# The seam between two transformer blocks: a ring of staging tiles, earlier reordered copies, and zero stores in another stage

## The chip, the cores and the metric

The kernel runs on one NeuronCore of a Trainium2 chip. A NeuronCore has a matrix engine (TensorE; PE in the profile, PEld for its weight loads), three engines for everything else (VectorE = DVE, ScalarE = ACT, GpSimd = POOL) and SyncE (SP), which here only issues transfers; ACT issues some as well. [...] The metric is device time in microseconds (us); lower is better.

## The reference, cut to what matters

One sequence of 512 tokens, 1024 wide, runs through a first network of two layers and then a hybrid layer, all in float32. What lies around the change:

```python
x = first_block(...)            # each layer ends: x = x + sigmoid(norm(x) @ Wg) * (p[i] @ Wp); then a norm
h = rms_norm_2(x, norm_g)       # the hybrid layer ("second block")
proj = h @ w_in                 # q, k, v of a sparse attention, and r, k, v, wd, ad, gate of an RWKV-7 mixer
p = p + shift_mu * (prev - p)   # token shift: prev is p one token earlier; for r, k, v, wd, ad
w = w0 + tanh(wd) @ w_up        # low-rank decay, rank 64
a = sigmoid(a0 + ad @ a_up)     # low-rank learning rate, rank 64
state = state * w_t + (state @ -kk_t) (kk_t * a_t) + v_t k_t      # per token, 8 heads of 64 x 64
```

The recurrence over tokens is computed in chunks of 64; within a chunk it needs the inverse of a unit triangular matrix per head.

## The kernel before, in words

Every float32 product is made of three products of halves: a weight unit is loaded by SP (`fetch`, line 162), rounded by ACT to `whi` (line 147), and the rest `wlo` is taken by DVE or POOL (line 148, by `N.lo`). Activations are split likewise into a high and a low tile. Lines 188 to 190 are the matmuls of `cols` (output transposed), line 205 those of `rows`.

**Token order.** The first block keeps its tokens in a permuted order (token mod 8 outermost), the second needs them in natural order. `natural` (line 322) makes reordered copies of the activations: 16 copies of 128x512, eight on ACT and eight on DVE (line 330).

**Stage A, the end of the first block** (lines 1526 to 1529, inside the `with` of pool `pn1`, for the second layer): after the last norm, `rwkv_proj_first` projects r, k, v of heads 0 to 3 (`hh` = 0) in permuted order, six passes of 48 matmuls. Each pass is evacuated by ACT (line 796), scaled by mu on DVE (797) and subtracted on POOL (798) into two large tiles, and eight stores of 384 KB (line 812) write them to the DRAM scratch `d_raw[0]`, undoing the permutation. Then `rwkv_lowrank` multiplies out the low-rank inputs (`cols` of `r_wa`), reorders and shifts them (lines 752 to 758), and for decay and learning rate and four token tiles does a float32 matmul over 65 rows (64 plus a row of ones; 769), tanh on ACT (771), a scaling on DVE (773) and a store on ACT's queue to `d_low` (774), with two output tiles in turn. r of heads 4 to 7 (`hh` = 1) follows.

**Stage B, the start of the second block** (lines 1540 to 1554): `rwkv_consts` loads two constants (728), casts them (730), clears a tile (733), and stores it eight times as zeros into the scratch `d_t` (736), which later holds the block inverses with zeros around them. k and v of heads 4 to 7 follow, then `natural`, then eight calls of `rwkv_local` (two halves of the heads, four token tiles), the local part of each chunk: each loads `low` from `d_low` (837) and r, k, v from `d_raw` (841), rounds the decay (221, `rt_lh`) and begins its matmuls with the cumulative sums into the banks `xa` (865). All of them read scratch that stage A wrote.

**The solve** (`rwkv_solve`, line 957): 31 steps of a forward substitution on DVE, 54 pairs of a product (967) and a subtraction (969), then four stores to `d_t` (972), which `rwkv_applied` loads back (995) for its matmuls (1003). `products` (line 1581) is the rest of the second block's matmul work: sparse-attention keys, gates, and query rows (`nsa_rows`, whose transposes are line 1229 and whose low parts DVE takes at line 1233).

**What sets the order.** The program is written with a tile framework that puts each engine's instructions in order itself: it picks what is ready in its own model of time, and among ready ones what the program emits first. So work emitted late can run early. On the chip every engine then runs its list strictly in order. A tile of a pool with `bufs` = n waits until the tile n allocations earlier is no longer in use; memory of a closed pool is waited for tile by tile.

## Time and profile before

| | |
|---|---|
| median of 3 runs | 1230.6 us (1230.04 to 1232.56) |
| the profiled execution | 1231.49 us |
| its span in the trace | 1229.7 us |
| mean granted TensorE clock | 0.969 of full speed |
| PE busy | 1141.6 us (93%) |
| DVE, ACT, POOL busy | 847.8, 623.7, 401.8 us |

The span is the traced part of one execution; 1.8 us of its time lie around it. Matmuls are pipelined and overlap in the listing, so a matmul's pace is read from the distance of starts, not from its duration. Where a row ends in brackets, they hold the engine's idle time before it and what ended it. In timelines of SP and ACT, "SPq" and "ACTq" rows are transfers being issued.

### The profile page before, as it was taken

The page shows a single profiled execution, that of the slowest core. Times are in us where ns is not written, and L with a number is a line of the kernel's source. Part 1 is how long each engine was busy: PE and PEld are TensorE (multiplying, and loading weights), DVE is VectorE, ACT ScalarE, POOL GpSimd, SP SyncE. Part 2 cuts the span into 40 slices and gives each one's busy share as a digit, 9 for nine tenths or more (in the row PEclk, how much of TensorE's full clock was granted, in tenths as well). Part 3 has the DMA queues.
Part 4 walks back from the last instruction along what each step waited for, and adds up shares of the span by engine and source line. Part 5 has one row for each costly group of instructions (what it writes and reads, how often), then busy time and mean ns, then how long its engine had stood idle before and what let it go on. Part 6 is the DMA issues. An engine that isn't in the chain of part 4 may idle for free.

```text
span 1229.7 us, 20522 instructions
## 1 busy us (share of the span) xinstructions
PE 1141.6 (93%) x7176; PEld 1001.5 (81%) x7176; DVE 847.8 (69%) x2097; ACT 623.7 (51%) x1355; POOL 401.8 (33%) x553
## 2 busy tenths in 40 slices
PE   7999999998999989999999999798989799899995
PEld 6898989887889768887877797788889688798884
DVE  6566666657677977886676763398885924788846
ACT  5566565635533566556565543433543223267832
POOL 0021211111200465674311011263444523357841
PEclk9999999999999999999999999899788979999998
DMA  6333333314233210210142436766657543712501
GB/s 247 116 104 103 104 98 95 99 53 141 88 102 90 82 35 1 69 38 32 52 146 66 149 107 205 239 225 180 192 167 175 162 137 103 241 45 78 189 35 69
DMA packets 87041, 143.26 MB, mean 116 GB/s; under 512 B 21525, under 2 KB 52245, under 8 KB 86938
## 3 DMA queue, kind: packets, MB, share of 16 engines
q1 hardware_dynamic: 72344, 133.49, 34.3%
q10 hardware_dynamic: 14018, 6.36, 2.0%
q0 software_dynamic: 576, 2.10, 0.6%
q8 instruction: 57, 0.93, 0.3%
q14 instruction: 46, 0.38, 0.1%
HBM read 114.12 MB, written 27.79 MB: 115 GB/s over the span
## 4 chain that ended last, share of the span: by engine, by line
PE 61%; DVE 18%; DMA 6%; ACT 6%; issue 5%; POOL 3%; SPq 2%; ACTq 0%; DVEq 0%; POOLq 0%
PE mm L205 24%; PE mm L188 5%; PE mm L189 5%; PE mm L190 5%; PE sc L205 3%; PE mm L216 2%; PE u L677 1%; PE tr L492 1%; DVE KT L967 1%; PE tr L670 1%; DVE big L969 1%; PE ch L1003 1%; PE tr L318 1%; DMA rkv<-d_raw 1%; PE u L205 1%
## 5 line engine op out<-in xcount | busy, mean ns | idle before, releaser
L205 PE MATMUL mm<-whi,act 128*128 128x256 f32 (+2 forms) x1344 | 357.4, 324 | 8.7 <-DVE x L347 3.3
L205 PE MATMUL mm<-wlo,act 128*128 128x256 f32 (+2 forms) x896 | 287.5, 321 | 0.4 <-POOL wlo L148 0.4
L205 PEld LDWEIGHTS mm<-whi,act 128*128 128x128 f32 x1344 | 240.9, 195 | 30.2 <-DVE x L347 5.6
L205 PEld LDWEIGHTS mm<-wlo,act 128*128 128x128 f32 x896 | 174.9, 195 | 10.3 <-POOL wlo L148 0.6
L147 ACT CAST whi<-wraw 128x1024 fp32r<-128x1024 f32 (+1 forms) x128 | 133.3, 1043 | 91.5 <-PE mm L205 36.8
L205 PE MATMUL mm<-whi,half 128*128 128x256 f32 (+1 forms) x448 | 145.6, 326 | 3.6 <-DVE half L222 3.6
L148 DVE TENSOR_TENSOR wlo<-wraw,whi 128x1024 fp32r<-128x1024 f32 x87 | 109.7, 1263 | 52.0 <-ACT whi L147 50.0
L148 POOL TENSOR_TENSOR wlo<-wraw,whi 128x1024 fp32r<-128x1024 f32 (+2 forms) x41 | 99.6, 2434 | 132.0 <-DVE rs_y L237 69.9
L188 PE MATMUL mm<-act,whi 128*128 128x512 f32 x312 | 125.4, 402 | 2.7 <-DVE b_qn L547 2.7
L190 PE MATMUL mm<-act,wlo 128*128 128x512 f32 x312 | 124.4, 399 | 0.0
L205 PEld LDWEIGHTS mm<-whi,half 128*128 128x128 f32 x448 | 87.8, 196 | 10.2 <-DVE half L222 4.5
L484 POOL TENSOR_SCALAR a_P<-a_P,a_rd 128x256 f32<-128x256 f32 x64 | 32.9, 517 | 156.6 <-DVE a_rd L483 143.9
L189 PE MATMUL mm<-half,whi 128*128 128x512 f32 x200 | 79.1, 396 | 0.0
L188 PEld LDWEIGHTS mm<-act,whi 128*128 128x128 f32 x312 | 59.6, 191 | 14.4 <-issue 3.6
L190 PEld LDWEIGHTS mm<-act,wlo 128*128 128x128 f32 x312 | 59.5, 191 | 12.0
L663 POOL TENSOR_SCALAR b_P<-b_P,b_rd 128x512 f32<-128x512 f32 x64 | 45.5, 715 | 54.8 <-DVE b_rd L662 44.2
L660 ACT ACTIVATE b_P<-sc,b_mn 128x512 f32<-128x512 f32 x64 | 44.1, 690 | 21.5 <-DVE b_mn L657 13.5
L657 DVE TENSOR_REDUCE b_mn<-sc 128x1 f32<-128x512 f32 x64 | 43.5, 684 | 10.9 <-PE sc L655 10.4
L478 DVE CUSTOM_DVE_ANT_0 a_P<-sc,a_bias 128x256 f32<-128x256 f32 x64 | 26.1, 422 | 34.7 <-PE tr L492 20.1
L222 DVE TENSOR_TENSOR b_pl<-tr,b_ph 128x512 fp32r<-128x512 f32 x64 | 43.3, 683 | 6.0 <-ACT b_ph L221 5.3
L1359 POOL TENSOR_SCALAR n_P<-n_P,b_rd,n_gl 128x128 f32<-128x128 f32 (+3 forms) x64 | 39.0, 616 | 25.5 <-DVE b_rd L1357 6.4
L189 PE MATMUL mm<-act,whi 128*128 128x512 f32 x112 | 45.3, 404 | 0.0
(391 smaller groups left out, 2836.5 us busy)
## 6 DMA issues: line engine op xcount, KB each, us to landing
wraw<-in_wstream SPq DMA_DIRECT2D x133, 512.0 KB, 3.6
a_bias<-in_bias SPq DMA_DIRECT2D x16, 384.0 KB, 3.0
rkv<-d_raw SPq DMA_DIRECT2D x16, 384.0 KB, 4.9
d_raw<-act SPq DMA_DIRECT2D x8, 384.0 KB, 5.7
xf<-x SPq DMA_DIRECT2D x4, 512.0 KB, 3.7
d_low<-low ACTq DMA_DIRECT2D x8, 256.0 KB, 2.5
d_t<-rkv SPq DMA_DIRECT2D x8, 256.0 KB, 4.1
low<-d_low SPq DMA_DIRECT2D x8, 256.0 KB, 3.3
```

The lines of the kernel that those rows point to most:

```text
L147: nc.scalar.copy(hi[:, :m], raw[:, :m])
L148: self.lo.tensor_tensor(lo[:, :m], raw[:, :m], hi[:, :m].bitcast(F32), op=OP.subtract)
L188: nc.tensor.matmul(ps, lhsT=wh[:, kt], rhs=ah[:, kt], start=kt == 0, stop=False)
L189: nc.tensor.matmul(ps, lhsT=wh[:, kt], rhs=al[:, kt], start=False, stop=False)
L190: nc.tensor.matmul(ps, lhsT=wl[:, kt], rhs=ah[:, kt], start=False, stop=kt == KT - 1)
L205: nc.tensor.matmul(ps, lhsT=l, rhs=r, start=i == 0, stop=i == len(ops) - 1)
L222: (eng_lo or nc.vector.tensor_sub)(lo, src, hi.bitcast(F32))
L484: nc.gpsimd.tensor_scalar(w, w, rd, 0.5, op0=OP.mult, op1=OP.mult)
L657: nc.vector.tensor_reduce(mn, ps, axis=AX.X, op=OP.max, negate=True)
L660: nc.scalar.activation(pt, ps, AF.Exp, bias=mn, scale=1.0, accum_out=den)
L663: nc.gpsimd.tensor_scalar(pt, pt, rd, 0.5, op0=OP.mult, op1=OP.mult)
L1359: nc.gpsimd.tensor_scalar(w, w, rd, st["gl"][:, b, gc:gc + 1], op0=OP.mult, op1=OP.mult)
```

## The change

- `rwkv_proj_first` is gone. All passes of heads 0 to 3 and of r of heads 4 to 7 use one ring `pp` of four tiles of 128x512 in `pn1` (two per pass; the name is that of a ring of the gate stage, now shared). Each pass issues its own four stores of 128 KB: 24 for heads 0 to 3 in place of eight of 384 KB.
- `natural` runs right after the projections of heads 0 to 3 are emitted. The low rank, and all of heads 4 to 7, read the natural-order copies; stores of heads 4 to 7 go to contiguous rows.
- The low rank: its loads and constant rows are emitted ahead of the `r_wa` product; the shift is one ACT and one DVE instruction on the product in PSUM; the products run over 128 rows (64 of data, one of ones, the rest zeros, cleared on POOL); three output tiles in turn.
- The zeros are cleared on POOL and stored from `zero_inverses`, called in the first layer's gate loop (`ple` of layer 0) at its second half, token tile 0.
- `rwkv_solve` is a generator: four steps are emitted after each of the first products.

```diff
-        zero = pool.tile([P, 768], F32, name="rkv", bufs=4)
-        nc.vector.memset(zero, 0.0)
+
+    def zero_inverses(self, pool):
+        nc = self.nc
+        zero = pool.tile([P, 512], F32, name="zero", bufs=1)
+        nc.gpsimd.memset(zero, 0.0)
         for t in range(TT):
             for h in range(2):
-                nc.sync.dma_start(out=self.head_rows(self.d_t, t, 4 * h, 4), in_=zero[:, :512].rearrange("p (h n) -> p h n", h=4))
+                nc.sync.dma_start(out=self.head_rows(self.d_t, t, 4 * h, 4), in_=zero.rearrange("p (h n) -> p h n", h=4))
...
-        ps = self.cols(("r_wa",), act)
-        raw, d = buf[:, 0], buf[:, 1]
-        nc.scalar.copy(raw.rearrange("p (r t c) -> p t c r", r=8, t=TT), ps.rearrange("p (t c r) -> p t c r", t=TT, r=8))
...
-        nc.vector.tensor_sub(d[:, 1:], raw[:, :S - 1], raw[:, 1:])
-        nc.vector.tensor_scalar(d[:, 0:1], raw[:, 0:1], -1.0, None, op0=OP.mult)
-        nc.vector.scalar_tensor_tensor(d, d, mu, raw, op0=OP.mult, op1=OP.add)
-
+        rest = self.small.tile([P, 1], F32, name="wa_rest", bufs=1)
+        nc.vector.tensor_scalar(rest, mu, -1.0, 1.0, op0=OP.mult, op1=OP.add)
+        ms = []
         for j, (up, row) in enumerate((("decay_up", "decay_w0"), ("iclr_up", "iclr_a0"))):
+            m, one = buf[:, 3 + 2 * j], 64 - 64 * j
+            nc.gpsimd.memset(m[64 - 64 * j:128 - 64 * j], 0.0)
+            nc.sync.dma_start(out=m[64 * j:64 * j + 64], in_=self.a[up])
+            nc.sync.dma_start(out=m[one:one + 1], in_=bass.AP(tensor=self.a[row].tensor, offset=self.a[row].offset, ap=[[S, 1], [1, S]]))
+            l = buf[:, 2 + 2 * j]
+            nc.gpsimd.memset(l[64 - 64 * j:128 - 64 * j], 0.0)
+            nc.gpsimd.memset(l[one:one + 1], 1.0)
+        ps = self.cols(("r_wa",), act)
+        d = buf[:, 0]
+        nc.scalar.mul(d, ps, rest)
+        nc.vector.scalar_tensor_tensor(d[:, 1:], ps[:, :S - 1], mu, d[:, 1:], op0=OP.mult, op1=OP.add)
+
+        for j in range(2):
             l, m = buf[:, 2 + 2 * j], buf[:, 3 + 2 * j]
...
+            nc.scalar.activation(l[w], d[w], AF.Tanh if j == 0 else AF.Copy)
             for t in range(TT):
                 ps = self.bank("sc")
-                nc.tensor.matmul(ps, lhsT=l[0:65, t * P:t * P + P], rhs=m[0:65], start=True, stop=True)
-                th = buf[:, 6 + t % 2]
+                nc.tensor.matmul(ps, lhsT=l[:, t * P:t * P + P], rhs=m, start=True, stop=True)
+                th = buf[:, (1, 6, 7)[(4 * j + t) % 3]]
...
-                for t in range(2 * hh):
+                for t in range(2):
                     for d, a in zip(self.d_raw[hh], r):
-                        o = bass.AP(tensor=d.tensor, offset=d.offset + (1 + 16 * (2 * tp + t)) * 768 + 256 * n, ap=[[768, 16], [64 * 768, 8], [1, 256]])
+                        o = (1 + (16, P)[hh] * (2 * tp + t)) * 768 + 256 * n
+                        o = bass.AP(tensor=d.tensor, offset=d.offset + o, ap=[[[768, 16], [64 * 768, 8]], [[768, P]]][hh] + [[1, 256]])
                         nc.sync.dma_start(out=o, in_=a[:, t])
...
                 nc.vector.tensor_tensor(tv, tv, o, op=OP.subtract)
+            yield
...
+                        if (hf, t) == (1, 0):
+                            N.zero_inverses(pool)
...
-                    rest = N.rwkv_proj_first(act, N.rwkv_mu(pool, 0, 0, 3, "mu0"))
+                    ring = lambda n, tp: [pool.tile([P, 512], F32, name="pp", bufs=4).rearrange("p (t n) -> p t n", t=2) for _ in range(2)]
+                    N.rwkv_proj(act, 0, "rkv", N.rwkv_mu(pool, 0, 0, 3, "mu0"), ring)
+                    act = N.natural(act)
                     N.rwkv_lowrank(pool.tile([P, 8, S], F32, name="low", bufs=1), act)
-                    N.rwkv_proj(act, 1, "r", N.rwkv_mu(pool, 1, 0, 1, "mu1"), lambda n, tp: [a[:, tp] for a in rest])
+                    N.rwkv_proj(act, 1, "r", N.rwkv_mu(pool, 1, 0, 1, "mu1"), ring)
...
-                act = N.natural(act)
...
-            N.rwkv_solve(chn, *sv)
+            solve = N.rwkv_solve(chn, *sv)
...
             for n, _ in enumerate(products()):
+                for _ in range(4 if n < 9 else 0):
+                    next(solve, None)
                 tail(n)
```

## Rows read from the trace of the kernel before

**Rows 1.** Busy time by stretch; columns: us, five engines, granted clock, DMA share, GB/s
```profile
720.00:743.00 23.00, 23.00 (x194) 23.00 (x192) 10.47 (x11) 8.25 (x11) 6.08 (x4) 1.00 0.44 131
...
787.00:793.00 6.00, 0.00 (x0) 0.00 (x0) 0.00 (x0) 0.35 (x2) 0.00 (x0) 0.87 0.80 246
...
797.00:937.00 140.00, 128.69 (x938) 118.82 (x938) 114.89 (x286) 60.88 (x191) 66.72 (x76) 0.87 0.60 187
```

**Rows 2.** Timeline of PE around 787 us: first matmul after the gap, and the pace
```profile
793.11 0.58 PE L865 MATMUL xa<-rt_lh,tri 128*128 128x256 f32 x1 [6.81 <-ACT rt_lh L221]
793.49 0.41 PE L205 MATMUL mm<-wlo,act 128*128 128x256 f32 x1
...
797.97 0.41 PE L205 MATMUL mm<-wlo,act 128*128 128x256 f32 x1
```

**Rows 3.** Timeline of SP, 774 to 789 us
```profile
774.63 0.33 SPq L686 DMA_DIRECT2D k_k<-in_k_k  x1
780.54 6.34 SPq L736 DMA_DIRECT2D d_t<-rkv  x8
...
788.65 0.43 SPq L837 DMA_DIRECT2D low<-d_low  x1
```

**Rows 4.** Timeline of ACT, 764 to 780 us
```profile
764.74 0.33 ACTq L774 DMA_DIRECT2D d_low<-low  x1
...
769.27 0.60 ACT L771 ACTIVATE low<-sc 128x512 f32<-128x512 f32 x1 [2.92 <-DMA d_low<-low]
770.03 1.20 ACT L330 CAST act<-half 128x512 fp32r<-128x512 f32 x1 [0.16 <-DMA d_raw<-act]
...
771.13 7.63 ACT L330 CAST act<-half 128x512 fp32r<-128x512 f32 x7
```

**Rows 5.** Timeline of PE, first matmuls of stage B
```profile
769.92 0.38 PE L205 MATMUL mm<-whi,act 128*128 128x256 f32 x1 [2.39 <-ACT low L771]
...
770.98 0.40 PE L205 MATMUL mm<-whi,half 128*128 128x256 f32 x1
...
773.95 0.41 PE L205 MATMUL mm<-wlo,act 128*128 128x256 f32 x1
```

**Rows 6.** Groups by line, 713 to 770 us: count, busy us, mean ns, idle before
```profile
L798 POOL TENSOR_TENSOR act<-act,act 128x512 f32<-128x512 f32 x8 | 11.2, 1399 | 77.1 <-DVE act L797 42.7 <-DVE rs_t L245 34.3
...
L769 PE MATMUL sc<-low 65*128 65x512 f32 x16 | 8.0, 598 | 0.4 <-ACT low L771 0.4
...
L797 DVE TENSOR_TENSOR act<-mm,mu 128x512 f32<-128x512 f32 x7 | 4.8, 688 | 4.8 <-ACT act L796 4.8
...
L796 ACT COPY act<-mm 128x512 f32<-128x512 f32 x7 | 4.1, 586 | 7.9 <-PE mm L205 7.9
```

**Rows 7.** Line 802's stores of 128 KB: issue ns min/median/max, time to landing
```profile
L802 SPq DMA_DIRECT2D d_raw<-act x8: 518/556/616, 757.7 to 767.6; - x8
...
DMA to landing us min/median/max: 2.3/3.7/7.1
```

**Rows 8.** SP's own waits, 690 to 1010 us: total, times, longest
```profile
SPq L162 <- DVE wlo L148: 19.2, 6, 7.8
```

**Rows 9.** Busy time in the first layer's gate stage, columns as in rows 1
```profile
320.00:330.00 10.00, 10.00 (x50) 8.38 (x49) 3.34 (x5) 4.47 (x9) 2.58 (x2) 1.00 0.01 2
```

**Rows 10.** Timelines of DVE, POOL and PE during the solve
```profile
956.88 0.47 DVE L967 TENSOR_TENSOR KT<-big,big 128x160 f32<-128x160 f32 x2
957.26 2.67 DVE L969 TENSOR_TENSOR big<-big,KT 128x160 f32<-128x160 f32 x2
...
957.31 2.52 POOL L148 TENSOR_TENSOR wlo<-wraw,whi 128x1024 fp32r<-128x1024 f32 x1 [4.84 <-ACT whi L147]
...
983.73 1.09 PE L1229 MATMUL mm<-ident,st 128*128 128x128 f32 x4 [8.35 <-DVE half L1233]
```

**Rows 11.** The chain that ended last: start us, us, what; around the solve
```profile
930.46 1.04 PE mm L1150 x4
...
988.33 6.83 DMA big<-d_t
```

More of the change, by code (lines that the diff above doesn't have):

```diff
@@ L755, in rwkv_lowrank @@
                                               ap=[[1, P], [1, 1]]))
-        nc.vector.tensor_sub(d[:, 1:], raw[:, :S - 1], raw[:, 1:])
-        nc.vector.tensor_scalar(d[:, 0:1], raw[:, 0:1], -1.0, None, op0=OP.mult)
-        nc.vector.scalar_tensor_tensor(d, d, mu, raw, op0=OP.mult, op1=OP.add)
+        rest = self.small.tile([P, 1], F32, name="wa_rest", bufs=1)
+        nc.vector.tensor_scalar(rest, mu, -1.0, 1.0, op0=OP.mult, op1=OP.add)
+        ms = []
         for j, (up, row) in enumerate((("decay_up", "decay_w0"), ("iclr_up", "iclr_a0"))):
-            l, m = buf[:, 2 + 2 * j], buf[:, 3 + 2 * j]
-            nc.scalar.activation(l[0:64], d[64 * j:64 * j + 64], AF.Tanh if j == 0 else AF.Copy)
-            nc.vector.memset(l[64:65], 1.0)
-            nc.sync.dma_start(out=m[0:64], in_=self.a[up])
-            nc.sync.dma_start(out=m[64:65], in_=bass.AP(tensor=self.a[row].tensor, offset=self.a[row].offset,
-                                                        ap=[[S, 1], [1, S]]))
+            m, one = buf[:, 3 + 2 * j], 64 - 64 * j
[10 more added lines that the diff above has]
+        for j in range(2):
+            l, m = buf[:, 2 + 2 * j], buf[:, 3 + 2 * j]
+            w = slice(64 * j, 64 * j + 64)
+            nc.scalar.activation(l[w], d[w], AF.Tanh if j == 0 else AF.Copy)
             for t in range(TT):
                 ps = self.bank("sc")
-                nc.tensor.matmul(ps, lhsT=l[0:65, t * P:t * P + P], rhs=m[0:65], start=True, stop=True)
-                th = buf[:, 6 + t % 2]
+                nc.tensor.matmul(ps, lhsT=l[:, t * P:t * P + P], rhs=m, start=True, stop=True)
+                th = buf[:, (1, 6, 7)[(4 * j + t) % 3]]
                 nc.scalar.activation(th, ps, AF.Tanh, scale=0.5)
@@ L798, in rwkv_proj @@
                 nc.gpsimd.tensor_tensor(r[0], r[0], r[1], op=OP.subtract)
-                for t in range(2 * hh):
+                for t in range(2):
                     for d, a in zip(self.d_raw[hh], r):
-                        o = bass.AP(tensor=d.tensor, offset=d.offset + (1 + 16 * (2 * tp + t)) * 768 + 256 * n, ap=[[768, 16], [64 * 768, 8], [1, 256]])
+                        o = (1 + (16, P)[hh] * (2 * tp + t)) * 768 + 256 * n
+                        o = bass.AP(tensor=d.tensor, offset=d.offset + o, ap=[[[768, 16], [64 * 768, 8]], [[768, P]]][hh] + [[1, 256]])
                         nc.sync.dma_start(out=o, in_=a[:, t])
-    def rwkv_proj_first(self, act, mu):
-        raw = [self.act_tile(self.act, j, F32).rearrange("p k n -> p (k n)") for j in range(2)]
-        full = [a[:, :TT * 768].rearrange("p (t n) -> p t n", t=TT) for a in raw]
-        self.rwkv_proj(act, 0, "rkv", mu, lambda n, tp: [a[:, 2 * tp:2 * tp + 2, 256 * n:256 * n + 256] for a in full])
-        for t in range(TT):
-            for d, a in zip(self.d_raw[0], full):
-                o = bass.AP(tensor=d.tensor, offset=d.offset + (1 + 16 * t) * 768, ap=[[768, 16], [64 * 768, 8], [1, 768]])
-                self.nc.sync.dma_start(out=o, in_=a[:, t])
-        return [a[:, TT * 768:].rearrange("p (a t n) -> p a t n", a=2, t=2) for a in raw]
     def rwkv_params(self, pool, hh):
```

## The prediction

> **What bounds the kernel now.** I read the busy time by stretch first, then PE's timeline in the stretches where PE is not full, then the lists of the engines named there. In stage A PE is full: 194 matmuls in 23.0 us at full clock, 0.119 us each, with every other engine under half busy [rows 1]. So in stage A PE is the pace, and work of other engines hides. At the seam there are two holes. PE's first matmul of stage B waits 2.39 us for the low rank's tanh on ACT, whose PSUM bank it inherits, and that tanh had waited 2.92 us for a store to free its output tile [rows 4, 5]. Then PE stands still 6.81 us for `rt_lh`, the first instruction of `rwkv_local` [rows 2]: between 787 and 793 us no engine but ACT does anything [rows 1]. The reader is to see in SP's list why: `low` is issued at 788.65, behind the eight zero stores that occupy SP from 780.54 for 6.34 us, and these start only at 780.54 although the transfer before them went out at 774.63 [rows 3], since DVE clears their tile behind its share of the reordered copies. [...]
>
> Behind the seam, from 797 to 937 us, PE is busy for 128.7 of 140 us and DVE for 114.9 [rows 1]; both matter, and PE draws on attention work that is emitted late and needs nothing of the local part. Then DVE is given to the solve, and PE waits once more, 8.35 us, for a DVE instruction that stands behind solve steps [rows 10].
>
> **The change part by part.** All against the profiled execution, 1231.49 us.
>
> *Zeros out of stage B.* The 6.81 us wait goes if `low` is there in time. Without the zeros SP goes from `k_k` (774.63, issue 0.33) to two parameter loads and `low`; before, those two took from 786.88 (end of the zeros) to 788.65, 1.8 us, so `low` is issued at 776.7 at the latest. From its issue to the first matmul passed 4.5 us (788.65 to 793.11) [rows 2, 3], so the matmul can go at 781.2 (the values it needs were on their way to `d_low` from 764.74 [rows 4]). PE reached that place at 786.3 (793.11 less 6.81): 5 us in hand. The wait goes entirely, and with it the slow stretch: from 793.49 to 797.97 are 21 steps of 0.213 us [rows 2] in place of 0.119, 2.0 us. Together **-8.8 us**. Late next is the second half of v's weights, whose cast on ACT stood behind `rt_lh`; as rounding on POOL takes 2.52 us [rows 10] after it, it could hold PE by up to about 1.5 us. I take none, since PE has the cumulative sums to go on with.
>
> *Three output tiles and the copies away from ACT.* The tanh that PE waited for was held 2.92 us by a store [rows 4]; a third tile takes that wait away, and the copies no longer stand in ACT's list between the last tanhs. The 2.39 us wait goes, and the slow stretch behind it (770.98 to 773.95, 14 steps, 1.3 us more than at full pace) [rows 5]: **-3.7 us**. Bounds 0 and 3.7; I take the whole, since two waits of the same length stand behind one another and one cause removes both.
>
> *Low rank over 128 rows.* 16 matmuls of 0.598 us [rows 6] stay 16, with the same 512 columns. No row shows this shape with 128 rows; the nearest, PE's other products, use 128 rows at no visible penalty. Bounds 0 and +1 us for all; I take 0. The evacuation of `r_wa` loses two DVE passes and a reordering on ACT, off PE's path while r of heads 4 to 7 runs. Six clears go to POOL, which is busy for 6 of 23 us there [rows 1]: 0.
>
> *Reordered copies in stage A.* Eight on ACT take 1.20 + 7.63 = 8.8 us [rows 4], DVE's eight less. ACT has 8.25 of 23 us in use between 720 and 743, so 14.7 us are free, and DVE 12.5 [rows 1]: they fit under PE, if they are put there. [...] Bounds 0 and +3 us (some two and a half copies of 1.2 us in PE's way); I take **+1 us**. Their cover is the six projections; what it costs without it is the first rival.
>
> *The ring.* 24 issues of 0.556 us [rows 7] replace eight, some 9 us more on SP, which is mostly idle in stage A. A ring tile turns over in 0.59 (ACT) + 0.69 (DVE) + 1.40 (POOL) [rows 6] + 4 issues of 0.556 + 3.7 to landing [rows 7] = 8.6 us. Two passes share the ring, so it is needed every 2 x 48 x 0.119 = 11.4 us: 2.8 us to spare, and one pass more (5.7 us) in the second PSUM bank. 0; the price if it fails is the second rival.
>
> *Zeros in the first layer's gate stage.* 6.34 us of SP and 2 MB of stores. There PE is full, the DMA share was 0.01 in one 10 us stretch, POOL 2.58 of 10 us busy [rows 9]. Bounds: 0, and 6.3 us if a weight load stands behind all eight when PE has no unit left. I take 0.
>
> *Solve steps interleaved in program order.* By position they move behind the key products, but the last key transposes already ran at 930.46, before the solve could start [rows 11], and gates and query rows are still emitted after it. For what runs beside the solve, nothing changes its rank. Bounds: -8.35 us (the whole wait of PE on DVE [rows 10]) and +3 us (a few key instructions ahead of solve steps); I take 0.
>
> *What the earlier start carries on.* PE gains 12.5 us up to the end of k and v, the local part's first matmul may come 11.9 us earlier at least, and as PE has 5 us in hand there, the solve should start a little earlier against PE's list than before. The 8.35 us wait shrinks by that: 0 to 5, I take **-2 us**.
>
> Sum: -8.8 - 3.7 + 1 - 2 = -13.5, from 1231.5 to 1218.0. The median of the runs stands 0.9 us under the profiled one, so 1217.1; I say **1217**. Behind the seam PE's amount of work is the same, so a shift there should arrive at the end.
>
> **The rivals.**
>
> *Copies late (about 1230).* The copies are emitted after the six projections. If the framework places them there, at 743 us, `r_wa` and all else needs them: 8.8 us of ACT with PE idle, then some 3 us of slow clock, and 12.5 - 11.8 leaves nothing. For it: in the old trace ACT ran them as one block [rows 4]. Against: the framework pulls ready work forward, as the key transposes, emitted behind the solve, that ran ahead of it [rows 11]. Decides at: first `r_wa` matmul after 745 us.
>
> *The ring stalls PE (about 1240): the slower side.* SP runs its list in order, and weight loads in it wait for DVE or POOL to free a raw tile, once 7.8 us [rows 8]. A ring store behind such a load makes the turnover 8.6 + 7.8 = 16.4 us against 11.4. Each pass would cost 2.5 us, eight passes 20, less the 5.7 of the spare bank, and each stall brings the slow clock: some 18 to 25 us of loss, against 12.5 gained, so 1236 to 1243. It decides from the point where stores stand more than 2.8 us (and the spare pass is used up) behind loads. Against: six such waits in the 320 us of that view, 3.2 us each on average, not far over the 2.8 us to spare.
>
> *The gain is eaten in the solve (about 1225).* A subtraction of the solve took 2.67 us beside POOL's `wlo`, 2.52 us, where its neighbour took 0.47 [rows 10]: 2.2 us lost per collision. If the shift puts three more weight units beside the solve, some 6.6 us go back: 1231.5 - 13.5 + 6.6 - 0.9 = 1224. [...]
>
> *The solve hole closes as well (about 1207).* If local part and solve run early enough that PE still has work beside them, the 8.35 us wait and the wait for the inverses (6.83 us in the chain [rows 11]) shrink together, by up to 12 us more: 1205 to 1210. For it: 5 us in hand. Against: DVE's order against PE's is fixed before the run.
>
> *The interleaving does nothing* is part of the forecast.
>
> **How the numbers follow.** Forecast, 1212 to 1222: 0.44. Hole closes as well: 0.18. Eaten in the solve or in a longer local part, 1222 to 1228: 0.15. Copies late: 0.11, of which half within 0.2%. Ring stalls, or zeros in the way of weights: 0.12. A measurement of this kernel tells 0.2% (2.5 us) from no change. Faster: 0.44 + 0.18 + 0.15 + 0.04 = 0.81; same 0.06; slower 0.13. The range for 8 in 10 leaves out the stalled ring above (0.12) and the lowest end of the closed hole, with the bounds at their best, below (0.05): 1203 to 1231.
>
> **What would show it.** In the changed profile: no `d_t` store by SP after 770 us; `low` issued within 5 us of `k_k`; first cumulative sum on PE without a wait; the reordered copies before 745 us; PE without a hole over 3 us between 745 and 790; first `rwkv_local` matmul 12 us earlier or more. The forecast is wrong if `r_wa` waits for a copy, if an evacuation on ACT waits for a DMA on `pp`, or if the PE waits of the solve grow by what the seam gave.

## The result, and the profile after

The changed kernel takes 1239.83 us (median of 13 runs, 1232.74 to 1243.4), the kernel before 1232.35 us beside it: a ratio of 1.0054, 95% interval [1.0033, 1.0075]. It is slower by half a per cent; faster was forecast. The profiled execution of after took 1239.37 us, its span is 1237.6 us (before: 1229.7), its mean granted clock 0.964 (before: 0.969).

To see where, I cut each trace where TensorE has begun as many of its 7176 matmuls as the kernel before had at 700, 780, 800, 960, 1000 and 1215 us. (The cuts are equal counts of matmuls, not the same instructions.)

| us per stage | to 700 | 700-780: stage A, start of k and v | 780-800: seam | 800-960: local part | 960-1000: solve | 1000-1215: recurrence, attention |
|---|---|---|---|---|---|---|
| before | 700.0 | 79.9 | 20.0 | 160.1 | 40.1 | 215.0 |
| after | +2.2 | 79.5 | 11.6 | 166.4 | 39.4 | 223.9 |
| after less before | +2.2 | -0.4 | -8.4 | +6.3 | -0.7 | +8.9 |

The sum is +7.9, the difference of the spans. (The +2.2 up to 700 us lie within what profiled runs differ by there, up to 4.8 us.) The seam closed as forecast, and more than all of it was lost again in two places behind it.

**What came as forecast.** Busy time by stretch of the changed kernel (columns as in rows 1):

```profile
720.00:743.00 23.00, 21.44 (x180) 21.24 (x179) 12.64 (x17) 11.53 (x13) 4.79 (x3) 1.00 0.60 167
787.00:793.00 6.00, 5.30 (x44) 5.21 (x44) 4.94 (x4) 2.41 (x4) 3.75 (x2) 1.00 0.97 292
797.00:937.00 140.00, 126.76 (x907) 116.42 (x906) 115.34 (x282) 58.62 (x187) 63.46 (x73) 0.87 0.54 168
```

The dead stretch from 787 to 793 us [rows 1] now has TensorE at work for 5.30 of 6 us. In SyncE's timeline no zeros stand between the parameters and `low` [rows 3]:

```profile
778.20 1.22 SPq L686 DMA_DIRECT2D k_k<-in_k_k  x1
...
782.33 0.38 SPq L836 DMA_DIRECT2D low<-d_low  x1
```

In TensorE's timeline the first matmul of stage B waits 0.45 us where it waited 2.39 [rows 5], and the first cumulative sum none where it waited 6.81 [rows 2]:

```profile
773.17 0.39 PE L205 MATMUL mm<-whi,act 128*128 128x256 f32 x1 [0.45 <-ACT low L780]
...
788.84 0.28 PE L864 MATMUL xa<-rt_lh,tri 128*128 128x256 f32 x1
...
808.41 2.10 PE L889 MATMUL x<-ident,rt 128*128 128x128 f32 x8 [3.91 <-DVE rt L891]
...
826.85 0.43 PE L927 MATMUL x<-rkv,am 128*128 128x64 f32 x2 [3.67 <-DVE abq L925]
```

**The first loss** is in the last two of these rows: TensorE, earlier at the local part, waits there for VectorE's first units. In stage 800-960 its idle time is 15.5 us (before 11.7) and the slow clock costs 18.0 us (before 15.6): +3.8 and +2.4, nearly the whole +6.3. What the slow clock costs is an estimate, here and below: half of TensorE's busy time in stretches granted 0.50. In one of them, 793.49 to 797.97 us [rows 2], starts are 0.213 us apart, and in 720 to 743 us, granted 1.00, 0.119 [rows 1]. VectorE's and GpSimd's timelines show what the first unit goes through:

```profile
799.57 4.76 POOL L148 TENSOR_TENSOR wlo<-wraw,whi 128x1024 fp32r<-128x1024 f32 x2
...
799.73 2.25 DVE L245 TENSOR_TENSOR l_t<-l_y 128x4 f32<-128x4 f32 x1
802.02 2.33 DVE L246 TENSOR_TENSOR l_t<-l_t,l_h 128x4 f32<-128x4 f32 x1
...
805.74 0.16 DVE L245 TENSOR_TENSOR l_t<-l_y 128x4 f32<-128x4 f32 x1
805.93 0.16 DVE L246 TENSOR_TENSOR l_t<-l_t,l_h 128x4 f32<-128x4 f32 x1
```

Two operations on 128x4, which take 0.16 us some 6 us later, take 2.25 and 2.33 us beside two `wlo` on GpSimd: 4.3 us in a chain at whose end (`rt`) TensorE waits 3.91 us. This is the collision of rows 10, in the local part instead of the solve. That `wlo` is what holds them is read from the times alone; by what it would hold them was not shown.

But the kernel before pays the same price in the same chain, a few operations earlier in it. Its timelines of GpSimd, VectorE and TensorE:

```profile
804.52 4.76 POOL L148 TENSOR_TENSOR wlo<-wraw,whi 128x1024 fp32r<-128x1024 f32 x2
...
804.62 2.33 DVE L236 TENSOR_SCALAR l_i<-l_ss 128x4 int32<-128x4 int32 x1
...
806.98 2.32 DVE L237 TENSOR_SCALAR l_y<-l_i 128x4 int32<-128x4 int32 x1
...
812.19 0.44 PE L890 MATMUL x<-ident,rt 128*128 128x128 f32 x2 [0.52 <-DVE rt L892]
```

From the first cumulative sum to the first transposes of `rt` pass 19.1 us in the kernel before (793.11 to 812.19) and 19.6 us in the changed one (788.84 to 808.41). So the collision is not what the change added. The chain keeps its length, and TensorE, without the slow stretch behind the old hole (from 793 to 798 us the kernel before has 23 matmuls at a granted clock of 0.50, the changed one 45 at 1.00), is through with its other work sooner and waits 3.91 us for the chain's end where it waited 0.52. What the collision is worth shows in a later run: in e5 only one operation of the chain is held (2.33 us), the same way takes 16.5 us (786.33 to 802.85), and the wait is 1.42 us.

**The second loss** comes behind the solve. Its wait is shorter than before, 6.05 us for 8.35 [rows 10], but that brings nothing: in stage 1000-1215 TensorE's idle time is 14.8 us (before 12.0) and the slow clock costs 8.5 us (before 1.4). Over all kernels whose list has the order of the kernel before, the slow clock costs 0 to 8.4 us in this stage, so the +8.9 of this one pair of traces is more than the order explains. Here the lists differ: ScalarE's timeline at the end of the solve has a weight cast (981.88) ahead of the stores of the inverses, which in the kernel before stood behind them.

```profile
981.39 0.58 ACT L1232 CAST half<-mm 64x512 fp32r<-64x512 f32 x1 [0.54 <-DVE half L1233]
981.88 1.05 ACT L147 CAST whi<-wraw 128x1024 fp32r<-128x1024 f32 x1
...
987.05 3.40 ACTq L972 DMA_DIRECT2D d_t<-big  x4
990.54 2.11 ACTq L995 DMA_DIRECT2D big<-d_t  x1
```

The change edits nothing there; the framework put the tail of every engine's list in another order. I call the order of the kernel before **tail A** and that of the changed kernel **tail B**. The expectations below name the tail for thirteen of the runs e5 to e18, from lists read before the run, and each trace has the tail named: TensorE ran its list in the order given. SyncE's list shows that the order is kept even where that costs: before, the load of `k_a` goes out 12.3 us after that of `k_k` (786.92 for 774.63), behind the zeros that wait for their tile until 780.54; in e1, without them, 0.4 us after it (776.56 for 776.19). The two tails can be told apart in the trace of any variant: behind the last matmul of `rwkv_local` TensorE does 1817 to 1819 matmuls in tail A, 1789 to 1792 in tail B. In the thirteen kernels with tail A the last 1780 matmuls of TensorE stand in one and the same order. Tail B is no single order: e2 and e11 have that of after, while e6, e9, e10 and e17 differ from it in some 650 of the 1780 places.

### The profile page after: what moved, and what is told of

The parts are those of the page before. It is cut to its first block, busy times and chain, and to the rows that moved or that the text cites. A ratio compares the mean times of both kernels' runs of the same rounds, so it can differ in the third digit from the quotient of the medians.

```text
span 1237.6 us, 20562 instructions
## 1 busy us (share of the span) xinstructions
PE 1150.6 (93%) x7176; PEld 1010.7 (82%) x7176; DVE 855.6 (69%) x2093; ACT 621.2 (50%) x1355; POOL 411.1 (33%) x560
## 4 chain that ended last, share of the span: by engine, by line
PE 67%; DVE 15%; DMA 5%; issue 4%; ACT 4%; POOL 3%; SPq 1%; ACTq 0%; POOLq 0%; DVEq 0%
PE mm L205 26%; PE mm L188 5%; PE mm L189 5%; PE mm L190 5%; PE mm L216 3%; PE sc L205 3%; DMA wraw<-in_wstream 2%; PE u L677 1%; PE tr L492 1%; PE tr L670 1%; PE u L1373 1%; DVE KT L966 1%; PE ch L1003 1%; PE tr L318 1%; ACT whi L147 1%
## 5 line engine op out<-in xcount | busy, mean ns | idle before, releaser
L205 PE MATMUL mm<-whi,act 128*128 128x256 f32 (+2 forms) x1440 | 370.0, 324 | 11.5 <-DVE st L407 3.2
L205 PEld LDWEIGHTS mm<-whi,act 128*128 128x128 f32 x1440 | 254.5, 196 | 35.2 <-DVE x L347 3.8
L148 POOL TENSOR_TENSOR wlo<-wraw,whi 128x1024 fp32r<-128x1024 f32 (+2 forms) x41 | 97.1, 2375 | 121.1 <-DVE rs_y L237 70.0
L188 PE MATMUL mm<-act,whi 128*128 128x512 f32 x312 | 125.9, 404 | 2.7 <-DVE b_qn L547 2.7
L205 PE MATMUL mm<-whi,half 128*128 128x256 f32 (+1 forms) x352 | 116.7, 332 | 3.1 <-DVE half L222 3.1
L484 POOL TENSOR_SCALAR a_P<-a_P,a_rd 128x256 f32<-128x256 f32 x64 | 33.0, 518 | 156.6 <-DVE a_rd L483 144.0
L189 PE MATMUL mm<-half,whi 128*128 128x512 f32 x192 | 76.1, 396 | 0.0
L205 PEld LDWEIGHTS mm<-whi,half 128*128 128x128 f32 x352 | 68.6, 195 | 8.7 <-DVE half L222 4.0
L657 DVE TENSOR_REDUCE b_mn<-sc 128x1 f32<-128x512 f32 x64 | 43.5, 684 | 12.2 <-PE sc L655 11.7
L189 PE MATMUL mm<-act,whi 128*128 128x512 f32 x120 | 49.1, 409 | 0.0
L1355 ACT ACTIVATE n_P<-n_P,b_mn 128x128 f32<-128x128 f32 (+3 forms) x64 | 35.7, 560 | 25.2 <-DVE b_mn L1352 15.3
```

What stands on the lines that cost most here:

```text
L148: self.lo.tensor_tensor(lo[:, :m], raw[:, :m], hi[:, :m].bitcast(F32), op=OP.subtract)
L188: nc.tensor.matmul(ps, lhsT=wh[:, kt], rhs=ah[:, kt], start=kt == 0, stop=False)
L189: nc.tensor.matmul(ps, lhsT=wh[:, kt], rhs=al[:, kt], start=False, stop=False)
L205: nc.tensor.matmul(ps, lhsT=l, rhs=r, start=i == 0, stop=i == len(ops) - 1)
L657: nc.vector.tensor_reduce(mn, ps, axis=AX.X, op=OP.max, negate=True)
L1355: nc.scalar.activation(w, w, AF.Exp, bias=mn, scale=-1.0, accum_out=den)
```

## The experiments

Eighteen runs, each over five rounds beside the kernel before; ratios are to its runs, with the 95% interval.

| run | median us | ratio | tail |
|---|---|---|---|
| after | 1239.83 | 1.0054 [1.0033, 1.0075] | B |
| e1 zeros moved only | 1231.52 | 0.9995 [0.9972, 1.0019] | A |
| e2 after, solve at once | 1234.55 | 1.0031 [1.0006, 1.0056] | B |
| e3 interleaving only | 1232.82 | 1.0010 [0.9987, 1.0032] | A |
| e4 after, zeros back | 1227.11 | 0.9968 [0.9943, 0.9993] | A |
| e5 after, one store back | 1226.30 | 0.9953 [0.9935, 0.9971] | A |
| e6 after, six stores back | 1236.27 | 1.0034 [1.0013, 1.0055] | B |
| e7 as e5, old low rank | 1231.61 | 0.9994 [0.9975, 1.0013] | A |
| e8 as e5, copies on GpSimd | 1226.50 | 0.9957 [0.9935, 0.9979] | A |
| e9 third tile only | 1236.14 | 1.0007 [0.9981, 1.0033] | B |
| e10 after, copies on GpSimd | 1237.68 | 1.0035 [1.0011, 1.0060] | B |
| e11 after, loads on SyncE | 1234.30 | 1.0016 [0.9994, 1.0038] | B |
| e12 zeros moved, third tile | 1228.79 | 0.9967 [0.9948, 0.9986] | A |
| e13 after, two tiles | 1231.70 | 0.9999 [0.9974, 1.0024] | A |
| e14 as e5, loads on SyncE | 1223.21 | 0.9923 [0.9897, 0.9948] | A |
| e15 before, loads on SyncE | 1225.84 | 0.9961 [0.9940, 0.9982] | A |
| e16 before, sixteen stores | 1242.83 | 1.0080 [1.0050, 1.0110] | A |
| e17 before, twelve stores | 1236.69 | 1.0023 [1.0002, 1.0044] | B |
| e18 three small edits | 1222.63 | 0.9905 [0.9881, 0.9928] | A |

Stages of some of them, cut as above:

| us per stage | 700-780 | 780-800 | 800-960 | 960-1000 | 1000-1215 |
|---|---|---|---|---|---|
| e1 | 79.8 | 18.1 | 158.9 | 40.6 | 220.6 |
| e5 | 79.5 | 10.7 | 164.4 | 40.3 | 216.6 |
| e7 | 83.9 | 13.5 | 160.6 | 37.2 | 215.9 |
| e9 | 75.7 | 11.5 | 166.3 | 39.9 | 222.8 |
| e12 | 75.7 | 20.0 | 156.6 | 39.7 | 214.8 |
| e13 | 79.5 | 14.2 | 163.7 | 38.6 | 219.7 |
| e16 | 79.9 | 10.7 | 176.3 | 41.6 | 216.1 |
| e17 | 79.9 | 10.7 | 167.0 | 40.1 | 217.2 |

The seam, too, has two orders. In e4, e6, e9, e16 and e17 the framework put 70 more matmuls (the second half of v's weights) ahead of the first cumulative sum. In them any wait for `rt_lh` falls behind the 800 us cut, so 10.7 or 11.5 in the second column does not mean that the hole is gone; there the second and third columns are to be read together.

### One part alone, and one part undone (e1 to e4)

e1 and e3 put one part into the kernel before, e2 and e4 take one out of the changed kernel.

```diff
@@ e1: before, with zero_inverses as in the change
+                        if (hf, t) == (1, 0):
+                            N.zero_inverses(pool)
@@ e2: after
             solve = N.rwkv_solve(chn, *sv)
+            for _ in solve:
+                pass
@@ e3: before, rwkv_solve as a generator
             for n, _ in enumerate(products()):
+                for _ in range(4 if n < 9 else 0):
+                    next(solve, None)
@@ e4: after, the stores again in rwkv_consts
-                        if (hf, t) == (1, 0):
-                            N.zero_inverses(pool)
```

e1: 

> The kernel before with one part of the change alone: the zeros for the inverses are stored in the first layer. Theory T1 (what the seam gains is kept unless something else takes it back; the change lost it through the copies in the last norm and through the solve spread between the products): the time is some 9 us under the kernel before, near 1223, with the gap of 6.8 us at the seam gone and a shift of about -9 from there to the end. Rival T2 (the local part is bound by its own chain of loads, buffers and VectorE/GpSimd, so a start that comes earlier is lost before the solve): the shift is -9 at 800 us, -2 or less by 850 us, and the time is that of the kernel before within 2 us.

e2: 

> The changed kernel, but the block inverses are emitted in one piece ahead of the products, as before. T1: the solve and with it the recurrence start earlier, the 6 to 8 us that the changed kernel loses between 1000 and 1140 us are gone, near 1232. T2, under which the recurrence's delay comes from the local part's end: within 2 us of the changed kernel, near 1239. A third theory T3 (the interleaving does fill PE's hole in the solve, and without it the products come late): 3 to 6 us slower than the changed kernel, near 1244.

e3: 

> The kernel before with the interleaved block inverses alone. T1: the recurrence comes 4 to 8 us later and the time is near 1238. T2: within 2 us of the kernel before. T3: 3 to 8 us faster than the kernel before, near 1226, by the 8.35 us gap in the solve.

e4: 

> The changed kernel, but the zeros are stored at the seam again, as before. T1: the seam's gap comes back in full, about 9 us slower than the changed kernel, near 1248. T2: the shift at 800 us is +9 against the changed kernel, is down to 2 us by 850 us, and the time is that of the changed kernel within 2 us.

e1 came out as T2 has it: nothing gained. But the hole at the seam did not go, as both theories supposed; it changed its cause. ScalarE's and TensorE's timelines of e1:

```profile
791.10 0.40 ACT L221 CAST rt_lh<-low 128x256 fp32r<-128x256 f32 x1 [8.12 <-DMA low<-d_low]
791.41 1.04 ACT L147 CAST whi<-wraw 128x1024 fp32r<-128x1024 f32 x1
```

```profile
792.50 0.80 PE L205 MATMUL mm<-whi,act 128*128 128x256 f32 x2 [5.41 <-ACT whi L147]
```

SyncE issues the first `low` at 777.68, but the second at 784.51; ScalarE waits 8.12 us for the second, and v's weight cast stands behind that wait. Stage 780-800 takes 18.1 us instead of 20.0.

e3 and e2 show that the interleaving costs or brings nothing in the kernel before, and at most about 5 us in the changed one, where the intervals overlap (1.0031 and 1.0054). e2 keeps tail B, so T1's reason for the late recurrence falls; T3 falls with e3, which gains nothing by it. e4 fell out of every theory: with the zeros back at the seam the kernel is some 11 us faster than the changed one. The seam's hole did not come back with them, since v's second half runs ahead of it; TensorE's timeline of e4:

```profile
795.29 0.39 PE L861 MATMUL xa<-rt_lh,tri 128*128 128x256 f32 x1 [0.50 <-ACT rt_lh L221]
```

And its list has tail A. So the next theory, T4: what matters is which tail the framework deals out.

### Near twins with the two tails (e5 to e10, e12, e13)

Each kernel was chosen by its lists so that two that hardly differ have different tails.

```diff
@@ e5 (k = 7) and e6 (k = 2): after, stores k to 7 at the seam, the others in the first layer
+        for j in range(k, 8):
+            nc.sync.dma_start(out=self.head_rows(self.d_t, j // 2, 4 * (j % 2), 4), in_=...)
...
+                if 2 * t + h < k:
@@ e8 (from e5) and e10 (from after): natural
-        engines = iter(TT * (nc.vector.tensor_copy, nc.vector.tensor_copy, nc.scalar.copy, nc.scalar.copy))
+        engines = iter(TT * (nc.gpsimd.tensor_copy, nc.gpsimd.tensor_copy, nc.scalar.copy, nc.scalar.copy))
@@ e9 (from before) and e12 (from e1)
-                th = buf[:, 6 + t % 2]
+                th = buf[:, (0, 6, 7)[(4 * j + t) % 3]]
@@ e13: after
-                th = buf[:, (1, 6, 7)[(4 * j + t) % 3]]
+                th = buf[:, (6, 7)[(4 * j + t) % 2]]
```

e7 is e5 with `rwkv_lowrank` of the kernel before, on the natural-order copies (a plain copy of the product in place of the reordering one).

e5: 

> The changed kernel, with the last of the eight zero stores back at the seam and seven in the first layer. In its lists the engines' order from the end of the local part on is that of the kernel before, not that of the changed kernel. Theory T4 (what the change gives back is not a wait at the seam but another order of the tail, from 947 us on, which the framework deals out as soon as its model sees the local part end earlier; by the shift after 1000 us it is worth 5 to 9 us): some 6 to 10 us faster than the changed kernel, 1229 to 1233, with the shift between 1000 and 1150 us gone. Rival T5 (storing zeros in the first layer costs by itself, in the first layer's or later transfers): seven eighths of that cost stay, so within 2 us of the changed kernel, 1237 to 1240.

e6: 

> The changed kernel, with six of the eight zero stores back at the seam and two in the first layer. In its lists the tail is of the changed kernel's kind (the first inverses are stored behind one more weight cast on ScalarE). T4: 5 to 9 us slower than the run with one store back, 1235 to 1240, though six stores stand where the kernel with all eight took 1227. T5: most of the zeros' cost is gone, 1228 to 1231.

e7: 

> As the run with one store back, but with the old low-rank part (65 rows, two output tiles, loads and shift in the old order); the tail is of the kind of the kernel before. If the third tile took away the 2.39 us wait and its slow stretch, as predicted, this is 3.7 us slower than the run with one store back. If early copies alone did that, within 1.5 us of it, and no wait of over 1 us for the low rank's tanh before k and v.

e8: 

> As the run with one store back, but VectorE's eight reordered copies run on GpSimd; the tail is of the kind of the kernel before. If the 3.7 us that the changed kernel loses between 700 and 740 us come from the copies between the last norm's steps on VectorE, at least 2 us of them come back and the time is 2 to 4 us under the run with one store back. If they come from ScalarE's copies, or if copies on GpSimd hold VectorE up as long, no gain: within 1.5 us, or slower.

e9: 

> The kernel before with one edit: three output tiles in the low rank in place of two, so that the tanh need not wait for a store. In its lists the tail is of the changed kernel's kind (two kinds are told apart by ScalarE's list: whether the weight cast after the last key casts stands ahead of the stores of the inverses or behind them). My prediction's step alone: 3.7 us under the kernel before, 1228.5. T4: the 2.39 us wait and its slow stretch go, but the tail costs 5 to 8 us from 960 us on, so 1 to 5 us slower than the kernel before, 1233 to 1237.

e12: 

> The kernel before with two edits: the third output tile, and the zeros stored in the first layer; the tail is of the kind of the kernel before. T4: the third tile's 3.7 us are kept here, 3 to 6 us under the kernel before, 1227 to 1229, and some 7 us under the run with the third tile alone. Rival: the local part takes back whatever the seam gives, within 2 us of the kernel before.

e10: 

> The changed kernel (all eight zero stores in the first layer) with VectorE's reordered copies on GpSimd; the tail is of the changed kernel's kind. It differs from the run with one store back and copies on GpSimd (1226.5) by one transfer's place. T4: 5 to 9 us slower than that run, 1232 to 1236. Rival (GpSimd's copies mend what the changed kernel loses): 1228 or less.

e13: 

> The changed kernel with two output tiles in the low rank in place of three; zeros as in the changed kernel, all in the first layer. The lists of the tail are of the kind of the kernel before. T4: the low rank's wait for a store may come back (up to 3.7 us), yet the tail gives 6 to 10 us, so some 3 to 8 us faster than the changed kernel, 1230 to 1235. Rival (the third tile only helps, the tail does not matter): 0 to 4 us slower than the changed kernel, 1240 to 1243.

Tail B goes with the longer time in five comparisons, as T4 has it (e5 and e10 came out some 2 to 3 us beyond the stated ranges, on the side that favours it). Tail B is slower than its twin with tail A by 1.0% (after, e5), 0.8% (e6, e5), 0.8% (e10, e8), 0.4% (e9, e12; here the intervals overlap a little) and 0.55% (after, e13). e6 and e5 differ in five stores besides, e9 and e12 in all eight, and e6 and e9 have the other order at the seam. e13 is the plainest: all zeros in the first layer, every other part of the change there, one buffer **less**, and some 7 us faster. T5 fell with e5: seven of eight zero stores in the first layer do no harm.

Busy time by stretch behind the solve, the changed kernel first, then e5:

```profile
1010.00:1040.00 30.00, 30.00 (x186) 27.33 (x186) 12.53 (x24) 9.78 (x17) 9.64 (x17) 0.89 0.23 71
1040.00:1160.00 120.00, 108.23 (x874) 97.38 (x875) 95.49 (x318) 64.16 (x171) 63.25 (x86) 0.96 0.44 137
```

```profile
1010.00:1040.00 30.00, 30.00 (x223) 26.83 (x221) 15.15 (x29) 9.93 (x18) 10.04 (x20) 1.00 0.35 104
1040.00:1160.00 120.00, 113.59 (x882) 102.14 (x882) 98.62 (x340) 73.84 (x194) 72.88 (x94) 0.96 0.43 136
```

With tail B TensorE is busy for 5.4 us less from 1040 to 1160 us, and has a lower mean clock from 1010 to 1040 (0.89 for 1.00). Over all profiled runs stage 1000-1215 takes 220.8 us on average with tail B (seven traces, after among them, 217.2 to 223.9) and 216.4 with tail A (thirteen, before among them, 213.3 to 220.6). Of the 4.4 us, 3.0 are idle time (13.8 for 10.8) and 1.8 slow clock (6.0 for 4.2), less 0.4 in the rest. A stretch that begins between 1013 and 1018 us and is granted 0.50 stands in six of the seven traces with tail B, all but e17, and in none of the thirteen with tail A.

e9 shows much of the case in one kernel: it takes away the wait that the prediction named, wins 4.2 us in stage 700-780 and, over the seam and the local part together, 2.3 (177.8 us from 780 to 960 for 180.1), and takes 7.8 more in the tail. The hole at the seam is not gone: `rt_lh` is still waited for, behind v's second half, and the wait for `rt` has grown. TensorE's timeline of e9:

```profile
797.14 0.39 PE L865 MATMUL xa<-rt_lh,tri 128*128 128x256 f32 x1 [2.54 <-ACT rt_lh L221]
...
812.60 0.69 PE L890 MATMUL x<-ident,rt 128*128 128x128 f32 x2 [4.06 <-DVE rt L892]
```

e7 has the whole low rank of the kernel before, two output tiles among it, with the copies out of the way: the wait is there in full, and stage 700-780 takes 83.9 us for e5's 79.5. e13 has two tiles as well, but the new low rank: the wait stays away, and the stage takes 79.5 us. So with the new low rank the third tile isn't what removes the wait. TensorE's timelines of e7, then e13:

```profile
774.77 0.38 PE L205 MATMUL mm<-whi,act 128*128 128x256 f32 x1 [2.68 <-ACT low L779]
```

```profile
775.76 0.39 PE L205 MATMUL mm<-whi,act 128*128 128x256 f32 x1 [0.45 <-ACT low L780]
```

e8 gains nothing by moving VectorE's copies: on GpSimd they leave stage 700-780 as it was (79.9 us for 79.5). TensorE's waits change places, though. Its wait for `hn` falls from 2.31 us in e5 to 1.14, while a wait for `half` grows from 1.20 to 2.14 and one of 1.42 us for a split on ScalarE is new. So which of the copies cost in stage A stays open.

### ScalarE and the loads of the inverses (e11, e14, e15)

```diff
-        nc.scalar.dma_start(out=T, in_=self.head_rows(self.d_t, t, 0, 8))
+        nc.sync.dma_start(out=T, in_=self.head_rows(self.d_t, t, 0, 8))
```

e11: 

> The changed kernel with the four loads of the inverses on SyncE's queue; TensorE's and VectorE's lists from the end of the local part on stay as they are, ScalarE's loses the four loads. If what the tail costs is ScalarE held by the first load's wait for the stores (the weight cast at 992.8 us behind it and TensorE's 3.2 us gap at 995), 3 to 4 us come back, near 1236. If it is the order in which the recurrence and the attention rows stand, within 1.5 us of the changed kernel, or slower where SyncE holds a load behind weights.

e14: 

> The run with one store back (1226.3), with the four loads of the inverses on SyncE's queue; tail of the kind of the kernel before, TensorE's and VectorE's lists unchanged. If ScalarE held by the load is a cost of the slower tail alone: within 1.5 us of 1226.3. If it is a cost of every tail: 3 to 5 us less, near 1222.

e15: 

> The kernel before with the four loads of the inverses on SyncE's queue. If ScalarE held by the load is a cost of the slower tail alone: within 1.5 us of the kernel before. If of every tail: 3 to 5 us faster.

All three come out 3 to 6 us under the kernel that they start from, whichever its tail (e11 and e14, the same edit on tail B and A, stand 0.9% apart). Only in e15 is this clear of noise by itself; the intervals of e11 and after, and of e14 and e5, overlap a little. So this is no cost of tail B, but one that every version carries. TensorE's timelines of e5, then e14, where the stores of the inverses begin at 979.45 and 979.25 us:

```profile
989.74 2.00 PE L1008 MATMUL ch<-act,big 128*128 128x128 f32 x8 [2.79 <-DMA big<-d_t]
```

```profile
987.27 1.16 PE L1008 MATMUL ch<-act,big 128*128 128x128 f32 x8
```

The product with the first inverses comes 2.5 us earlier; its wait of 2.79 us is gone, and so is the slow stretch behind it (2.00 us for eight matmuls, now 1.16). The load itself is issued 0.6 us earlier (981.61 for 982.22) and lands in 5.6 us for 7.5. ScalarE's next weight cast moves by 0.2 us only (982.82 for 983.05), so ScalarE held by the load, of which the expectations speak, is not what this pair shows; why the load lands sooner stays open.

### A longer hole, and the version that the runs point to (e16 to e18)

```diff
@@ e16: before, rwkv_consts (e17: [0, 1, 2, 3, 0, 1])
-        for t in range(TT):
+        for t in [0, 1, 2, 3, 0, 1, 2, 3]:
             for h in range(2):
                 nc.sync.dma_start(out=self.head_rows(self.d_t, t, 4 * h, 4), ...)
```

e18 is e12 with the loads of the inverses on SyncE's queue.

e16: 

> The kernel before with each of the eight zero stores at the seam issued twice; the tail is of the kind of the kernel before. My prediction's claim (a shift at the seam arrives at the end): about 6.3 us of SyncE more, 6 to 8 us slower, 1238 to 1240. Rival T2 (the local part is bound by its own engines and takes a shift at the seam back): the hole at the seam grows by 4 to 6 us, the stretch from 780 to 960 us by 2 us or less, and the time is within 2.5 us of the kernel before.

e17: 

> The kernel before with twelve zero stores at the seam in place of eight; the tail is of the changed kernel's kind. By the stores alone it stands between the kernel before and the run with sixteen. T4: the tail from 1000 us on takes 220 to 224 us in place of 215, and it is 3 to 8 us slower than the run with sixteen stores if that one keeps the time of before; in any case slower than the kernel before by 4 us or more.

e18: 

> The kernel before with three small edits: the third output tile, the zeros in the first layer, the loads of the inverses on SyncE's queue; the tail is of the kind of the kernel before. If the pieces add: 1228.8 less some 5, near 1224. If the loads gain nothing here: near 1229.

SyncE's and TensorE's timelines of e16:

```profile
780.61 13.66 SPq L736 DMA_DIRECT2D d_t<-rkv  x16
```

```profile
805.92 0.58 PE L865 MATMUL xa<-rt_lh,tri 128*128 128x256 f32 x1 [11.18 <-ACT rt_lh L221]
```

SyncE is held 7.3 us longer, the stages from 780 to 960 us together take 187.0 us for 180.1, TensorE's idle time in them is 30.8 us for 18.5, and the run comes out 0.8% slower (some 10 us): this longer hole arrives in full. So T2 as a limit of the local part is out. The shorter holes hardly arrive: from 780 to 960 the changed kernel takes 178.0 us, e1 177.0, e5 175.1, e9 177.8, e12 176.6, some 2 to 5 us under the kernel before. Even that is within what single traces differ by: e15, in which TensorE's order is that of the kernel before up to 921 us, takes 174.8 us there, with 9.4 us less of slow clock. TensorE's idle time from 780 to 960 is the steadier number: 18.5 us before, 20.6 in e15, 16.2 in the changed kernel, 19.5 in e1, 16.9 in e5, 22.3 in e9, 18.7 in e12. So of the 6.81 us wait that `low` caused, 2.3 us of idle time at most stay gone in these; other things (`whi`, VectorE's first unit) are nearly as late as `low` was.

e17 is a miss for T4: it has tail B, but with half of e16's extra stores it has less than half of its loss, and its tail took 217.2 us in the profile. So tail B's price isn't fixed. Nor does every longer hole arrive: e17's stores hold SyncE for 9.70 us (6.34 before), and yet from 780 to 960 it takes 177.7 us, with 20.7 us idle; v's second half, which it has ahead of the first cumulative sum, covers them.

e18 beats both kernels: 0.95% under the kernel before, with three small edits.

## Why the prediction was wrong

The step that failed is the last sentence of its sum: "Behind the seam PE's amount of work is the same, so a shift there should arrive at the end." The shift was there: at 800 us TensorE stood 12.5 us earlier against 760 (from 5.9 us late to 6.6 us early), the very 12.5 forecast. (The sign that the local part's first matmul comes 12 us earlier failed even so: it came 4.3 us earlier, 788.84 for 793.11, for TensorE was 5.9 us late at 760 us.) At 960 us 0.3 us of the shift were left, and at the end the kernel was 7.9 us late. It didn't arrive, because

1. what waited next was nearly as late: the local part took 6.3 us more, 3.8 of it idle time, with two waits for VectorE of 3.91 and 3.67 us, and 2.4 slow clock, which single traces differ by anyway;
2. the framework orders every list by its own model, in which an edit at the seam moves what is ready later. The changed kernel was dealt tail B. That the order of the tail costs the rest is borne out by the five pairs, not by a run that changes it alone. I had used the framework's freedom to argue that the copies would run early, and not asked what else it would deal anew.

The terms one by one:

- *Zeros, -8.8.* Right in size with all parts together (-8.4 in stage 780-800), mis-sized by itself: alone they gave 1.9 us there (e1), and with the third tile nothing (e12, 20.0 us). The prediction named the right successor, v's second weight cast, bounded it by 1.5 us and took none; it was 5.41 us. The hole also shrinks with the zeros left at the seam, where the framework puts v's second half ahead of it: to 0.50 us in e4 and 2.54 in e9.
- *Three tiles and copies, -3.7.* Right in size: 4.2 us in stage 700-780 (e9 and e12), by the tile alone, with the copies where they were. Copies away from ACT are not enough with the old low rank (2.68 us, e7), and with the new low rank the tile isn't needed (0.45 us with two, e13); which part of it does that is not shown.
- *Copies in stage A, +1, bounds 0 to 3.* It was +3.7 (the shift from 700 to 740 us). The +1 is shown by no run, nor is how many copies stand in TensorE's way; what the traces show is this: the wait for `hn` at 709.62 us grew from 1.39 to 2.29, a slow stretch follows it (granted 0.50 from 711.6 to 715.0 us), and at 731.37 TensorE waits 1.56 us for an evacuation on VectorE. In front of that evacuation stands not a copy but a weight's low part (`wlo`, 729.49, 1.23 us); VectorE's last copy was done at 727.08. The shift from 700 to 740 us, 3.6 to 4.1 us, stands in all kernels that have the copies early and in no other; but the same kernels have the ring, and no run parts the two.
- *Ring, low rank over 128 rows, zeros in the first layer: 0 each.* Not contradicted: no TensorE wait for a `pp` store, the matmul still 0.59 us, and e5 is among the fastest with seven stores in the first layer.
- *Interleaving, 0.* Right in the kernel before (e3, 1.0010).
- *Carried into the solve's wait, -2.* Right in size (8.35 to 6.05 us) by luck: 0.3 us of the shift were left to carry at 960 us, and the wait is 5.9 to 8.6 us over all traces. It was worth nothing at the end.

Of the rivals, the gain "eaten in the solve or in a longer local part" names the place of the first loss, in the local part, but not its mechanism: the collision that it reckons with is as dear in the kernel before. (In its row, 2.67 us are two subtractions together and 0.47 us two products; the 2.2 us lost stand.) None had the second. Two rivals reckon with a slow clock behind a stall. In both traces each wait of TensorE of over 2 us from 400 us on (six before, eight after) goes with a stretch granted 0.50, which begins between 4.5 us before the end of the wait and 2.3 us behind it; the 3 us that the rival of the late copies sets behind 8.8 us of idle PE are an estimate, beside the 1.3 us read behind a wait of 2.39 and the 2.0 behind one of 6.81. Copies late and the stalled ring did not happen: the last reordered copies ran at 725 to 727 us, and SyncE issued the stores as they came.

What stays open is which rows of tail B make its stage 1000-1215 longer: the idle time is spread over some ten waits of 0.3 to 2.3 us, one slow stretch recurs at 1013 to 1018 us, and no run changed that order alone. Open, too, is which of the parts in stage A costs the 3.7 us there.

## What to carry to other kernels

Where a framework orders the lists, compare the lists of both builds behind the edit before adding up waits: an edit that changes the order far behind it is priced by that order too, and a twin that differs in one harmless transfer tells the two apart. A hole closes only down to the next late thing, so list what is due within its width; that it opens fully when lengthened (e16) says nothing about closing it. Before a slow operation is called the cause of a wait, look for it in the kernel before as well. Try a load that must wait for stores on another queue than the one that issues the stores: here SyncE's in place of ScalarE's was worth some 5 us (e15).

## What was not expected of the hardware

The same kernel runs with and without certain slow stretches of TensorE, and its time follows: e4's runs with a mean granted clock of 0.972 to 0.976 took 1222.3 to 1227.4 us, those at 0.965 to 0.968 took 1229.9 to 1233.1. In the profiled runs of e1, e4, e5 and e7 a stretch of 10.2 us from 1041 to 1045 us on was granted 0.50; in those of before and e8, with tail A as well, there was none. Even to 700 us, where the lists are nearly the same, profiled runs differ by up to 4.8 us. A single trace is therefore no measure of a 5 us effect here; the verdicts above rest on 6 to 13 runs each.
